# Gains moved from the weight tiles to the activations, and weight tiles split in pairs

## The chip, the core and the metric

One Trainium2 chip, one of its cores. Five engines of the core work at the same time, each through its own instructions in a fixed order: the tensor engine (PE, with its weight loads PEld), the vector engine (DVE), the scalar engine (ACT), GpSimd (POOL) and SyncE (SP), which here issues every DMA. An engine whose next instruction waits for another engine, or for a DMA, does nothing in the meantime, even when later instructions could run. Data lies in HBM, in SBUF (128 partitions) and, for the tensor engine's results, in PSUM. The metric is the time of one execution on the device in microseconds (us); less is better.

## The reference

Two layers of a decoder on 256 tokens of width 2048, all in float32. Each layer is a mixer and an FFN, each between two RMS norms with gains:

```python
h = rms_norm(x, g_mix_pre)                    # x * rsqrt(mean x^2) * gain
proj = h @ w_in                               # 2048 x 11776
u_pool, u_conv, q, k, v, g_ret, gate_pre = jnp.split(proj, IN_OFFSETS, axis=-1)
y_pool = pool_mixer(u_pool, pool_w, pool_scale) @ w_pool_proj   # ends in "* pool_scale"
y_conv = conv_module(u_conv, ...) @ w_conv_proj
y_ret = retention(q, k, v, g_ret, positions, ret_gn_g) @ w_ret_proj   # ends in "* gn_g", silu(gate)
merged = gates[:, :, 0] * y_pool + gates[:, :, 1] * y_conv + gates[:, :, 2] * y_ret
x = x + rms_norm(merged @ w_out, g_mix_post)
h = rms_norm(x, g_ffn_pre)
a, b = jnp.split(h @ w_ffn_in, 2, axis=-1)    # 2048 x 11264
x = x + rms_norm((jax.nn.silu(a) * b) @ w_ffn_out, g_ffn_post)
```

Four of these gains stand directly ahead of a product with a weight matrix: `g_mix_pre`, `g_ffn_pre`, `pool_scale` and `ret_gn_g`. Such a gain has one factor for each row of the matrix, so it can go on the activation's column or on the weight's row.

## The kernel before, in words

The weights, 2048 tiles of 128 rows x 512 columns, are read once in the order in which they are used. `fetch` (line 602) brings two row tiles at a time (512 KB, one DMA) into one of 4 buffers `raw`. `load` (line 611) splits each tile into two parts in the narrower format float32r: ACT writes the high part `whi`, DVE the rest, `wlo`. Where the rows have a gain, ACT multiplies by it while it writes `whi` (line 623) and DVE does so while it subtracts (line 624); the other tiles take lines 620 and 621. 13 buffers of each part are kept.

The activations stand transposed, also split: `split` (line 122) makes a high part on ACT (line 124) and a rest on DVE (line 125) of four blocks of 128 x 128, a *quad*, which `transpose4` (line 128) has put into PSUM with four products by the identity. A float32 product is then three products, `multiply` (line 637): activation high with `whi` (line 648), high with `wlo` (line 649), low with `whi` (line 650). Each takes 128 tokens; the two halves of the tokens are called h = 0 and h = 1, and h = 1 follows 7 to 8 tiles behind h = 0 (`LAG`), so that what lies between two sub-layers for one half is done beside products of the other.

Between two sub-layers, `post_norm` (line 177) adds up squares, lets POOL make the factor `rpost` (lines 117 and 119), and DVE updates `x` in four blocks of 512 columns (line 185); each block is then transposed and split to a quad of the new `xT`. The conv, pooling and retention work is cut into small jobs that are put between the products.

The order on each engine is made by a scheduler from the program and its own estimates, except for the first 16 tiles (`begin`, line 661), where the program's order is kept for PE, ACT, DVE and SP; but instructions of later parts can still be placed among them. One of these is the conversion of the token positions, `posf` (line 210), for the rotary tables. Its input `posi` comes by two small DMAs (line 208). At the start, SP issues DMAs for `x`, the first weights, parameters (`par`), pooling tables (`dt`) and gains (`gp`). Eight are in flight at the most: from the ninth on, each DMA's issue waits until the one eight places before it has landed.

Of the kernel before, what the change touches and what calls it, by code (L numbers as in the profile page):

```python
# [37 lines left out]
WBUFS = 13  # L38
# [32 lines left out]
def trunk(ctx: ExitStack, tc: tile.TileContext, x, positions, g_mix_post, g_ffn_post, w_in, pool_w,  # L71
# [50 lines left out]
    def split(src):  # L122
        t = slot([P, 2, 4, P], F32R)
        act.copy(t[:, 0], src)  # L124
        dve.tensor_tensor(t[:, 1], src, t[:, 0].bitcast(F32), op=ALU.subtract)  # L125
        return t
# [25 lines left out]
    def pre_norm_quad(h, c):  # L152
        st["xT", h].append(split(transpose4(xs[h][:, c, :])))
# [15 lines left out]
    def post_collect(h, c, src, bc):  # L169
        """One 512 column block of a sub-layer's output: kept times its gain, squares summed."""  # L170
# [6 lines left out]
    def post_norm(h, final):  # L177
# [5 lines left out]
        def residual(c):  # L183
            xc = xs[h][:, c, :]
            dve.scalar_tensor_tensor(xc, ogs[c], r, xc, op0=ALU.mult, op1=ALU.add)  # L185
            if final:
                nc.sync.dma_start(out[0, h * P:(h + 1) * P, c * NB:(c + 1) * NB], xc)

        if final:
            for c in range(4):  # L190
                residual(c)
            return
        st["xT", h] = []
        residual(0)
        for c in range(4):
            defer(N_FIRST + N_STEP * c, pre_norm_quad, h, c)
# [131 lines left out]
    def pool_job(l, h):  # L328
# [21 lines left out]
        st["brT", 0, h] = [split(ps)]  # L350
        yield 1.4

    def ret_job(l, h, qd):
# [50 lines left out]
        st["brT", 2, h][qd] = split(transpose4(m))  # L404
# [111 lines left out]
    def ev_out(l, c):  # L516
        def f(h, ps):
# [3 lines left out]
            if c == 3:  # L521
                post_norm(h, False)
# [19 lines left out]
    def ev_ffn(l, c, part, last):  # L542
        def f(h, ps):
# [9 lines left out]
            if c == 3:  # L553
                post_norm(h, l + 1 == DEPTH)
        return f

# [4 lines left out]
    def add(w, r0, kt, c0, lhs, evac, gain=None, needs=()):  # L561
        chunks.append((w, r0, kt, c0, lhs, evac, gain, needs))

    for l in range(DEPTH):
        wi = w_in[l]
        gpre, gffn = par[l][:, C_GPRE:C_GPRE + 16], par[l][:, C_GFFN:C_GFFN + 16]
        add(wi, 0, 16, Q_POOL, "xT", ev_pool(l), gpre)
        for qd in range(2):
            add(wi, 0, 16, Q_V + qd * NB, "xT", ev_v(qd), gpre)
        for qd in range(2):  # L570
            add(wi, 0, 16, Q_Q + qd * NB, "xT", ev_rot("qT", qd), gpre)
        for qd in range(2):
# [29 lines left out]
    def fetch(i):  # L602
# [5 lines left out]
        for kk in range(LOAD):  # L608
            raws[i + kk] = raw[:, kk, :]
# [150 lines left out]
```

## Time and profile before

| | |
|---|---|
| median of 3 runs | 2905.14 us (2904.59 to 2905.62) |
| span of the profiled execution (the only time it has) | 2904.9 us |
| PE busy | 2882.4 us, 99% of the span |
| DVE busy | 1896.8 us, 65% |
| ACT busy | 1631.0 us, 56% |
| DMA | 190 GB/s in the mean |
| mean granted clock of the tensor engine | 0.999 |

A group's row gives line, engine, operation, tiles as "written<-read", shapes and count, then the busy time and the mean of one, then the idle time of that engine just before them and what ended most of it. The timeline gives start and duration of single instructions; two that follow each other on one engine overlap by some 0.1 us, so what an instruction costs its engine is the distance between two starts. The busy time of PE says little about what could be saved: its products overlap.

### The profile page before, as it was taken

Reading aid. Unit: us, or ns where it says so; the run is one execution under the profiler, and the core shown is the slowest. Engines: PE = TensorE matmul, PEld = TensorE weight load, DVE = VectorE, ACT = ScalarE, POOL = GpSimd, SP = SyncE. Lnnn points to the kernel's source line nnn. Section 1 sums busy time; section 2 is a strip of 40 time slices with the busy share of each in tenths; the row PEclk is TensorE's granted clock in tenths of the full one; section 3 lists DMA queues with packets and bytes.
Section 4 is the critical chain, followed back from the end, with each engine's and each line's share of the span. In section 5 each row is a group of like instructions: output and inputs, shape, how many; then the busy total and the mean of one; then the engine's idle time right before and its main releaser. Section 6 shows DMA issues by size and latency. Waiting matters only on the chain.

```text
span 2904.9 us, 36969 instructions
## 1 busy us (share of the span) xinstructions
PE 2882.4 (99%) x13072; PEld 2389.0 (82%) x13072; DVE 1896.8 (65%) x2925; ACT 1631.0 (56%) x2477; POOL 87.8 (3%) x94
## 2 busy tenths in 40 slices
PE   8999999999999999999999999999999999999998
PEld 7888888888888888888888888888888888888887
DVE  6667976666666555666566679766666665556655
ACT  6555556555655545555565555565565555455553
POOL 0000000110000000000000000001000000000000
PEclk9999999999999999999999999999999999999999
DMA  7666666656666656665666656666556665566654
GB/s 245 193 187 179 185 203 188 189 188 202 182 189 189 189 195 193 189 191 190 203 186 187 186 173 188 201 184 195 190 184 197 189 190 189 195 190 190 189 197 148
DMA packets 287689, 553.14 MB, mean 190 GB/s; under 512 B 17680, under 2 KB 18960, under 8 KB 287504
## 3 DMA queue, kind: packets, MB, share of 16 engines
q1 hardware_dynamic: 287504, 550.79, 62.7%
q8 instruction: 102, 1.67, 0.2%
q14 instruction: 83, 0.68, 0.1%
HBM read 548.62 MB, written 2.10 MB: 190 GB/s over the span
## 4 chain that ended last, share of the span: by engine, by line
PE 97%; DVE 1%; DMA 0%; POOL 0%; issue 0%; ACT 0%; SPq 0%; DVEq 0%; POOLq 0%; ACTq 0%
PE mm L650 32%; PE mm L648 32%; PE mm L649 32%; PE tp L131 2%; DVE wlo L624 0%; DVE x L185 0%; PE sc L387 0%; PE tp L379 0%; DMA x<-in_x 0%; PE sc L343 0%; DVE slot L175 0%; DMA dt<-in_bands 0%; POOL rpost_a L117 0%; POOL rpost L119 0%; PE sc L349 0%
## 5 line engine op out<-in xcount | busy, mean ns | idle before, releaser
L648 PE MATMUL mm<-whi,slot 128*128 128x512 f32 x4096 | 1606.9, 392 | 0.0
L650 PE MATMUL mm<-whi,slot 128*128 128x512 f32 x4096 | 1597.3, 390 | 0.0
L649 PE MATMUL mm<-wlo,slot 128*128 128x512 f32 x4096 | 1596.3, 390 | 0.0
L623 ACT ACTIVATE whi<-raw,par 128x512 fp32r<-128x512 f32 x1536 | 1110.0, 725 | 822.2 <-PE mm L650 787.4
L624 DVE SCALAR_TENSOR_TENSOR wlo<-raw,par,whi 128x512 fp32r<-128x512 f32 x1536 | 1162.0, 761 | 603.9 <-ACT whi L623 585.9
L650 PEld LDWEIGHTS mm<-whi,slot 128*128 128x128 f32 x4096 | 769.3, 188 | 161.0 <-DVE slot L125 0.6
L649 PEld LDWEIGHTS mm<-wlo,slot 128*128 128x128 f32 x4096 | 769.9, 188 | 156.1 <-DVE wlo L624 0.4
L648 PEld LDWEIGHTS mm<-whi,slot 128*128 128x128 f32 x4096 | 769.9, 188 | 155.8 <-ACT slot L124 0.7
L621 DVE TENSOR_TENSOR wlo<-raw,whi 128x512 fp32r<-128x512 f32 x512 | 355.3, 695 | 294.3 <-ACT whi L620 293.1
L620 ACT CAST whi<-raw 128x512 fp32r<-128x512 f32 x512 | 319.0, 623 | 332.8 <-DVE wlo L621 240.1
L301 DVE SCALAR_TENSOR_TENSOR slot<-slot,par,slot 128x252 f32<-128x252 f32 (+19 forms) x240 | 104.6, 466 | 0.4
L125 DVE TENSOR_TENSOR slot<-tp,slot 128x512 fp32r<-128x512 f32 x100 | 68.3, 687 | 24.0 <-ACT slot L124 23.9
L124 ACT CAST slot<-tp 128x512 fp32r<-128x512 f32 x100 | 57.5, 578 | 31.9 <-PE tp L131 31.8
L496 POOL TENSOR_TENSOR slot<-slot,tb 128x512 f32<-128x512 f32 x32 | 55.8, 1745 | 633.6 <-DVE tb L495 615.4
L117 POOL TENSOR_SCALAR rpost_a<-ssq_t 128x1 f32<-128x1 f32 x8 | 4.1, 513 | 1610.2 <-DVE ssq_t L179 1610.2
L483 ACT ACTIVATE sg<-mm,rstd 128x512 f32<-128x512 f32 x48 | 33.1, 690 | 15.0 <-PE mm L650 14.9
L529 DVE SCALAR_TENSOR_TENSOR sg<-mm,rstd,tb 128x512 f32<-128x512 f32 x44 | 32.9, 748 | 12.7 <-ACT tb L527 12.7
L131 PEld LDWEIGHTS tp<-ident,ta 128*128 128x128 f32 x272 | 34.0, 142 | 8.4
L131 PE MATMUL tp<-ident,ta 128*128 128x128 f32 x272 | 40.6, 271 | 0.0
L537 DVE SCALAR_TENSOR_TENSOR ta<-mm,rstd,sg 128x512 f32<-128x512 f32 x44 | 32.9, 747 | 9.6 <-PE mm L650 9.5
L527 ACT ACTIVATE tb<-mm,rstd 128x512 f32<-128x512 f32 x44 | 30.4, 690 | 14.1 <-PE mm L650 14.1
L131 PE MATMUL tp<-ident,x 128*128 128x128 f32 x128 | 20.6, 289 | 10.8 <-DMA x<-in_x 7.3
(104 smaller groups left out, 469.9 us busy)
## 6 DMA issues: line engine op xcount, KB each, us to landing
raw<-in_w_in SPq DMA_DIRECT2D x368, 512.0 KB, 3.7
raw<-in_w_ffn_in SPq DMA_DIRECT2D x352, 512.0 KB, 3.8
raw<-in_w_ffn_out SPq DMA_DIRECT2D x176, 512.0 KB, 3.6
raw<-in_w_out SPq DMA_DIRECT2D x64, 512.0 KB, 3.7
raw<-in_w_ret_proj SPq DMA_DIRECT2D x32, 512.0 KB, 4.1
raw<-in_w_pool_proj SPq DMA_DIRECT2D x16, 512.0 KB, 3.8
raw<-in_w_conv_proj SPq DMA_DIRECT2D x16, 512.0 KB, 4.2
dt<-in_decays SPq DMA_DIRECT2D x12, 256.0 KB, 4.0
```

What stands on the lines that cost most here:

```text
L124: act.copy(t[:, 0], src)
L125: dve.tensor_tensor(t[:, 1], src, t[:, 0].bitcast(F32), op=ALU.subtract)
L131: pe.transpose(tp[:, j, :], src[:, j * P:(j + 1) * P], ident)
L301: dve.scalar_tensor_tensor(acc[:, ct, s:], hT[:, ct, :SEQ - s], w[:, TAPS - 1 - s:TAPS - s], acc[:, ct, s:], op0=ALU.mult, op1=ALU.add)
L496: gp.tensor_tensor(m, m, t, op=ALU.add)
L620: act.copy(hi, raw)
L621: dve.tensor_tensor(lo, raw, hi.bitcast(F32), op=ALU.subtract)
L623: act.activation(hi, raw, ACT.Identity, scale=gain[:, k:k + 1])
L624: dve.scalar_tensor_tensor(lo, raw, gain[:, k:k + 1], hi.bitcast(F32), op0=ALU.mult, op1=ALU.subtract)
L648: pe.matmul(ps, ah, hi, start=(k == 0), stop=False)
L649: pe.matmul(ps, ah, lo, start=False, stop=False)
L650: pe.matmul(ps, al, hi, start=False, stop=(k == kt - 1))
```

## The change

Line numbers below are those of the changed kernel where they stand with rows of it.

1. **Gains go on the activations.** `split` takes a `gain`; where it has one, DVE first writes `u = src * gain` (128 x 512, one instruction, the gain repeated along the columns) into SBUF (line 127), and ACT (line 129) and DVE (line 130) then split `u`. This is so for the 32 quads of `xT` (8 at each of 4 sub-layers), for the 4 of the pooling branch and the 8 of the retention branch.
2. **Weight tiles are split in pairs.** `load` takes the whole of `raw`: one ACT copy (line 621) and one DVE subtraction (line 622) of 128 x 1024. There are 1024 of each in place of 2048.
3. **Buffers.** 7 blocks of two tiles of `whi` and of `wlo`, 14 tiles in place of 13. A block comes free when h = 1 has used both of its tiles.

```diff
-    def split(src):
+    def split(src, gain=None):
         t = slot([P, 2, 4, P], F32R)
+        if gain is not None:
+            u = t2("ta", 3, (P, 4, P))
+            dve.tensor_tensor(u, src, gain.unsqueeze(2).to_broadcast([P, 4, P]), op=ALU.mult)
+            src = u
         act.copy(t[:, 0], src)
         dve.tensor_tensor(t[:, 1], src, t[:, 0].bitcast(F32), op=ALU.subtract)
         return t
...
-    def load(i):
-        n, k = items[i]
-        gain = chunks[n][6]
+    def load():
+
+        i = loaded[0]
         if i not in raws:
             fetch(i)
         raw = raws.pop(i)
-        hi = wpool.tile([P, NB], F32R, name=nm("whi"), tag="whi", bufs=WBUFS)
-        lo = wpool.tile([P, NB], F32R, name=nm("wlo"), tag="wlo", bufs=WBUFS)
-        if gain is None:
-            act.copy(hi, raw)
-            dve.tensor_tensor(lo, raw, hi.bitcast(F32), op=ALU.subtract)
-        else:
-            act.activation(hi, raw, ACT.Identity, scale=gain[:, k:k + 1])
-            dve.scalar_tensor_tensor(lo, raw, gain[:, k:k + 1], hi.bitcast(F32), op0=ALU.mult, op1=ALU.subtract)
-        wt[i] = (hi, lo)
-
-    ahead = [WBUFS]
+        hi = wpool.tile([P, LOAD, NB], F32R, name=nm("whi"), tag="whi", bufs=WBLOCKS)
+        lo = wpool.tile([P, LOAD, NB], F32R, name=nm("wlo"), tag="wlo", bufs=WBLOCKS)
+        act.copy(hi, raw)
+        dve.tensor_tensor(lo, raw, hi.bitcast(F32), op=ALU.subtract)
+        for kk in range(LOAD):
+            wt[i + kk] = (hi[:, kk, :], lo[:, kk, :])
+        loaded[0] += LOAD
+
+    ahead = [LOAD * WBLOCKS]
...
     def load_ahead():
-        load_next(max(0, min(len(items), done[1] + ahead[0]) - loaded[0]))
+        while loaded[0] < min(len(items), done[1] // LOAD * LOAD + ahead[0]):
+            load()
```

The scheduler's order changes with it at a few places. **First, SP at the start**, from its thirteenth DMA on. Before (`raw_N` is a pair of weight tiles, `x_80` and `x_81` are h = 0 and h = 1 of `x`):

```order
L205 DMA par_83<-in_params 128x180
L607 DMA raw_182<-in_w_in 128x2x512
L167 DMA x_81<-in_x 128x512
L607 DMA raw_210<-in_w_in 128x2x512
L167 DMA x_80<-in_x 128x512
L607 DMA raw_244<-in_w_in 128x2x512
L167 DMA x_81<-in_x 128x512
L607 DMA raw_272<-in_w_in 128x2x512
L208 DMA posi<-in_positions 128x1 x2
```

and now:

```order
L210 DMA par_83<-in_params 128x180
L213 DMA posi<-in_positions 128x1 x2
L610 DMA raw_178<-in_w_in 128x2x512
L172 DMA x_81<-in_x 128x512
L511 DMA gp_5160<-in_g_mix_post 128x512
L610 DMA raw_204<-in_w_in 128x2x512
L172 DMA x_80<-in_x 128x512
```

The two DMAs of `posi` moved from behind the last weights of the start to the places right behind `par_83`, and the gains `gp` moved forward too.

**Second, DVE at the start.** Before, from its second computing instruction on (`tp` is a transposed quad in PSUM, `slot` a split one; `posf` comes as the twentieth row):

```order
L125 TENSOR_TENSOR slot_98<-tp_93,slot_98 128x512
L624 SCALAR_TENSOR_TENSOR wlo_102<-raw_88,par_82,whi_101 128x512
L624 SCALAR_TENSOR_TENSOR wlo_106<-raw_88,par_82,whi_105 128x512
L125 TENSOR_TENSOR slot_114<-tp_109,slot_114 128x512
L624 SCALAR_TENSOR_TENSOR wlo_122<-raw_91,par_82,whi_121 128x512
L624 SCALAR_TENSOR_TENSOR wlo_126<-raw_91,par_82,whi_125 128x512
L125 TENSOR_TENSOR slot_145<-tp_140,slot_145 128x512
```

and now:

```order
L127 TENSOR_TENSOR ta_99<-tp_93,par_82 128x512
L130 TENSOR_TENSOR slot_98<-ta_99,slot_98 128x512
L622 TENSOR_TENSOR wlo_104<-raw_88,whi_103 128x1024
L127 TENSOR_TENSOR ta_113<-tp_107,par_82 128x512
L130 TENSOR_TENSOR slot_112<-ta_113,slot_112 128x512
L215 CAST posf<-posi 128x2
L622 TENSOR_TENSOR wlo_122<-raw_91,whi_121 128x1024
L127 TENSOR_TENSOR ta_142<-tp_136,par_82 128x512
L130 TENSOR_TENSOR slot_141<-ta_142,slot_141 128x512
L622 TENSOR_TENSOR wlo_149<-raw_118,whi_148 128x1024
```

Each quad has a second DVE instruction, and `posf` moved from the twentieth row to the seventh, ahead of the second pair's `wlo`.

**Third, DVE between the first mixer and the first FFN**, from the last gain product of h = 0 on. Before (`x_80` is updated by columns of 512, `tp_6644` is the first transposed quad):

```order
L175 TENSOR_TENSOR slot_6414<-mm_6425,gp_6600 128x512
L179 TENSOR_REDUCE ssq_t_6605<-ssq_o_6039 128x1
L624 SCALAR_TENSOR_TENSOR wlo_6616<-raw_6591,par_82,whi_6615 128x512
L185 SCALAR_TENSOR_TENSOR x_80<-slot_6038,rpost_6609,x_80 128x512
L624 SCALAR_TENSOR_TENSOR wlo_6625<-raw_6622,par_82,whi_6624 128x512
L624 SCALAR_TENSOR_TENSOR wlo_6632<-raw_6622,par_82,whi_6631 128x512
L624 SCALAR_TENSOR_TENSOR wlo_6641<-raw_6638,par_82,whi_6640 128x512
L125 TENSOR_TENSOR slot_6649<-tp_6644,slot_6649 128x512
L185 SCALAR_TENSOR_TENSOR x_80<-slot_6038,rpost_6609,x_80 128x512
```

and now:

```order
L180 TENSOR_TENSOR slot_5474<-mm_5481,gp_5628 128x512
L184 TENSOR_REDUCE ssq_t_5633<-ssq_o_5163 128x1
L622 TENSOR_TENSOR wlo_5649<-raw_5646,whi_5648 128x1024
L190 SCALAR_TENSOR_TENSOR x_80<-slot_5162,rpost_5637,x_80 128x512
L622 TENSOR_TENSOR wlo_5661<-raw_5658,whi_5660 128x1024
L127 TENSOR_TENSOR ta_5670<-tp_5664,par_82 128x512
L190 SCALAR_TENSOR_TENSOR x_80<-slot_5162,rpost_5637,x_80 128x512
L622 TENSOR_TENSOR wlo_5684<-raw_5681,whi_5683 128x1024
L130 TENSOR_TENSOR slot_5669<-ta_5670,slot_5669 128x512
L127 TENSOR_TENSOR ta_5693<-tp_5687,par_82 128x512
L190 SCALAR_TENSOR_TENSOR x_80<-slot_5474,rpost_5637,x_80 128x512
```

A block of `wlo` and the new product `ta` now stand between two updates of `x_80`, and another block ahead of the quad's low part. On PE the first transposes of `x_80` there moved 7 products back, to 4 products ahead of the end of h = 1's sub-layer, and the second ones moved 2 products forward, ahead of the first product of the new sub-layer instead of behind its second. At the other two transitions both come to stand at the same places. Over the whole program PE keeps its products; their order differs at these places and, by single products, in the first 60 us.

More of the change, by code (lines that the diff above doesn't have):

```diff
@@ L37 @@
 LAG = 7
-WBUFS = 13
+WBLOCKS = 7
 SLOTS = 22
@@ L150, in tick, with pre_norm_quad @@
             fn(*args)
-    def pre_norm_quad(h, c):
-        st["xT", h].append(split(transpose4(xs[h][:, c, :])))
+    def pre_norm_quad(h, c, gain):
+        st["xT", h].append(split(transpose4(xs[h][:, c, :]), gain[:, 4 * c:4 * c + 4]))
     def pre_norm_rstd(h, ssq):
@@ L175, in post_collect, with post_norm @@
         dve.tensor_tensor(o, src, bc, op=ALU.mult)
-    def post_norm(h, final):
+    def post_norm(h, gain):
         tot = small("ssq_t", 1)
@@ L185, in residual @@
             dve.scalar_tensor_tensor(xc, ogs[c], r, xc, op0=ALU.mult, op1=ALU.add)
-            if final:
+            if gain is None:
                 nc.sync.dma_start(out[0, h * P:(h + 1) * P, c * NB:(c + 1) * NB], xc)
-        if final:
+        if gain is None:
             for c in range(4):
@@ L195, in post_norm @@
         for c in range(4):
-            defer(N_FIRST + N_STEP * c, pre_norm_quad, h, c)
+            defer(N_FIRST + N_STEP * c, pre_norm_quad, h, c, gain)
             if c < 3:
@@ L349, in pool_job @@
             pe.matmul(ps[:, g, :], pw[:, g, :], pT[:, g, :], start=True, stop=True)
-        st["brT", 0, h] = [split(ps)]
+        st["brT", 0, h] = [split(ps, par[l][:, C_PS:C_PS + 4])]
         yield 1.4
@@ L403, in ret_job @@
         yield WAIT
-        st["brT", 2, h][qd] = split(transpose4(m))
+        st["brT", 2, h][qd] = split(transpose4(m), par[l][:, C_GN + 4 * qd:C_GN + 4 * qd + 4])
         yield 1.2
@@ L521, in f @@
             if c == 3:
-                post_norm(h, False)
+                post_norm(h, par[l][:, C_GFFN:C_GFFN + 16])
         return f
@@ L553, in f @@
             if c == 3:
-                post_norm(h, l + 1 == DEPTH)
+                post_norm(h, par[l + 1][:, C_GPRE:C_GPRE + 16] if l + 1 < DEPTH else None)
         return f
@@ L588, in trunk @@
             for j in range(b0, b1):
-                add(w_ffn_in[l], 0, 16, j * NB, "xT", ev_a, gffn)
-                add(w_ffn_in[l], 0, 16, HIDDEN + j * NB, "xT", ev_b(j == b0), gffn)
+                add(w_ffn_in[l], 0, 16, j * NB, "xT", ev_a)
+                add(w_ffn_in[l], 0, 16, HIDDEN + j * NB, "xT", ev_b(j == b0))
             for c in range(4):
@@ L607, in fetch @@
         nc.sync.dma_start(raw, w[r:r + LOAD * P, c0:c0 + NB].rearrange("(k p) n -> p k n", p=P))
-        for kk in range(LOAD):
-            raws[i + kk] = raw[:, kk, :]
-    def load(i):
-        n, k = items[i]
-        gain = chunks[n][6]
+        raws[i] = raw
+    def load():
+        i = loaded[0]
         if i not in raws:
@@ L639, in multiply @@
         n, k = items[i]
-        w, r0, kt, c0, lhs, evac, gain, needs = chunks[n]
+        w, r0, kt, c0, lhs, evac, needs = chunks[n]
         if k == 0:
@@ L661, in begin @@
     def begin():
+        gain = par[0][:, C_GPRE:C_GPRE + 16]
         load_x(0, 0)
@@ L666, in begin @@
         fetch(2)
-        pre_norm_quad(0, 0)
-        load_next(2)
+        pre_norm_quad(0, 0, gain)
+        load()
         for c in range(4):
             if c == 0:
-                pre_norm_quad(1, 0)
+                pre_norm_quad(1, 0, gain)
             if c < 3:
@@ L675, in begin @@
                 load_x(1, c + 1)
-            load_next(2)
+            load()
             multiply(0)
@@ L680, in begin @@
             if c < 3:
-                pre_norm_quad(0, c + 1)
+                pre_norm_quad(0, c + 1, gain)
                 fetch(4 * c + 6)
-                load_next(2)
+                load()
             multiply(1)
             if c < 3:
-                pre_norm_quad(1, c + 1)
+                pre_norm_quad(1, c + 1, gain)
             for h in (0, 0, 1, 1):
@@ L695, in trunk @@
         begin()
-    ahead[0] = WBUFS
+    ahead[0] = LOAD * WBLOCKS
     defer(16, add_job, ("trig", 0), rotary_tables(), True)
```

30 lines of the change are left out of this document (12 added, 18 removed).

## The prediction

> **What bounds the kernel now.** I read the page's groups first, then the waits of PE, then the start and the first transition in the timeline.
>
> ```profile
> span 2904.9 us, 36969 instructions
> PE mm L650 32%; PE mm L648 32%; PE mm L649 32%; PE tp L131 2%; DVE wlo L624 0%; DVE x L185 0%; PE sc L387 0%; PE tp L379 0%; DMA x<-in_x 0%; PE sc L343 0%; DVE slot L175 0%; DMA dt<-in_bands 0%; POOL rpost_a L117 0%; POOL rpost L119 0%; PE sc L349 0%
> L648 PE MATMUL mm<-whi,slot 128*128 128x512 f32 x4096 | 1606.9, 392 | 0.0
> L623 ACT ACTIVATE whi<-raw,par 128x512 fp32r<-128x512 f32 x1536 | 1110.0, 725 | 822.2 <-PE mm L650 787.4
> L624 DVE SCALAR_TENSOR_TENSOR wlo<-raw,par,whi 128x512 fp32r<-128x512 f32 x1536 | 1162.0, 761 | 603.9 <-ACT whi L623 585.9
> L621 DVE TENSOR_TENSOR wlo<-raw,whi 128x512 fp32r<-128x512 f32 x512 | 355.3, 695 | 294.3 <-ACT whi L620 293.1
> L620 ACT CAST whi<-raw 128x512 fp32r<-128x512 f32 x512 | 319.0, 623 | 332.8 <-DVE wlo L621 240.1
> ...
> 1509.23 0.39 PE L648 MATMUL mm<-whi,slot 128*128 128x512 f32 x1
> 1510.59 0.39 PE L648 MATMUL mm<-whi,slot 128*128 128x512 f32 x1
> ...
> PE tp L131 <- DMA x<-in_x: 7.3, 2, 3.7
> PE tp L131 <- DVE x L185: 3.6, 6, 0.9
> PE sc L343 <- DMA dt<-in_bands: 1.7, 1, 1.7
> ```
>
> The chain that ends last is PE's three products, 96%. Six products lie between the two L648 rows, so one costs 1.36 / 6 = 0.227 us, and 3 x 4096 of them 2786 us of 2904.9. The split that the change makes cheaper is not on that chain: ACT idles 787 us in front of L623 because PE still holds the buffers, DVE idles behind ACT. PE's waits are 12.6 us in all. 7.3 is the first arrival of `x`, which stays. The 3.6 us are six waits at the three transitions (two each, 1.2 us). So the change cannot gain more than about 3.6 us, whatever it saves on DVE and ACT; it can lose where it makes PE wait anew. The span agrees with the median of the runs (2905.14) to 0.01%. A measurement of this kernel tells about 0.2% (5.8 us) from no change.
>
> **What is removed, and hidden.** 1536 + 512 splits on each engine become 1024 of 128 x 1024. No row has that shape; I extend rows:
>
> ```profile
> L457 DVE TENSOR_TENSOR tb<-mm,tr 128x256 f32<-128x256 f32 x16 | 6.6, 415 | 0.0
> L456 DVE TENSOR_TENSOR ta<-mm,tr 128x512 f32<-128x512 f32 x16 | 11.1, 691 | 6.9 <-PE mm L650 6.9
> L136 ACT ACTIVATE junk<-x 128x512 f32<-128x512 f32 x32 | 20.3, 633 | 6.4 <-DVE x L185 6.1
> L248 ACT ACTIVATE sin<-slot 128x128 f32<-128x128 f32 x1 | 0.3, 312 | 0.0
> L124 ACT CAST slot<-ta 128x512 fp32r<-128x512 f32 x4 | 2.6, 646 | 0.0
> ```
>
> DVE takes (691 - 415) / 256 = 1.08 ns a column, so 1024 columns take 695 + 512 x 1.04 to 1.08 = 1.23 us (bounds: 1.06 if the fixed part vanished, 1.39 if it doubled). ACT takes (633 - 312) / 384 = 0.84 ns a column: 623 + 428 = 1.05 us (bounds 0.99, 1.25). DVE's sum falls by 1536 x 0.761 + 512 x 0.695 - 1024 x 1.23 = 265 us, ACT's by about 354. Worth to the end: nothing, since PE's products hide it. Their cover is wide: a pair's buffers come free 4 tiles of both halves ahead of their next use, 24 products or 5.4 us, against 1.05 + 1.23 and one instruction in front on each engine, about 3.7. The 14 tiles in place of 13 let the first tile of a pair start when it did.
>
> **What is added: 44 products by the gain on DVE.** They read PSUM with a repeated factor, as L456 does: 0.69 us, 30 us in all. ACT then reads SBUF (646 ns). The 12 of pooling and retention lie beside PE's products; if they were late, each costs 0.7 us. The 32 of `xT` stand on a path that PE waits for.
>
> **The start: a wait that was harmless comes to the front.**
>
> ```profile
> 6.70 1.33 ACT L623 ACTIVATE whi<-raw,par 128x512 fp32r<-128x512 f32 x2 [1.31 <-DMA raw<-in_w_in]
> 9.61 0.33 SPq L205 DMA_DIRECT2D par<-in_params  x1
> 11.05 0.38 SPq L607 DMA_DIRECT2D raw<-in_w_in  x1
> 12.35 0.33 SPq L167 DMA_DIRECT2D x<-in_x  x1
> 19.22 0.94 SPq L208 DMA_DIRECT2D posi<-in_positions  x2
> ...
> DMA to landing us min/median/max: 2.6/4.9/7.1
> ...
> DMA to landing us min/median/max: 4.6/4.8/4.9
> ...
> 14.20 0.59 ACT L124 CAST slot<-tp 128x512 fp32r<-128x512 f32 x1 [2.88 <-PE tp L131]
> 15.07 0.48 PE L648 MATMUL mm<-whi,slot 128*128 128x512 f32 x1
> 15.38 0.39 PE L649 MATMUL mm<-wlo,slot 128*128 128x512 f32 x1
> 25.08 0.16 DVE L210 CAST posf<-posi 128x2 f32<-128x2 int32 x1
> 27.80 0.47 PE L648 MATMUL mm<-whi,slot 128*128 128x512 f32 x1
> ```
>
> The landing rows are of `par` (2.6 for the first, 7.1 for the one issued at 9.61, since the first was in use at 6.70) and of `posi`. Before, `posi` was issued at 19.2 and read at 25.08 without a wait. Now its two DMAs take the next two places behind `par`, where SP issued at 11.05 and 12.35, behind all the data of the start. `par` lands at 9.61 + 7.1 = 16.7; `posi`, behind it, between 12.35 + 4.6 = 16.95 and 12.35 + 7.1 = 19.45. I take 17.0, because `par`'s landing shows when that backlog is through. `posf` now stands on DVE ahead of the second pair's `wlo`, so DVE is blocked until then. Behind it wait that `wlo` (17.2 to 18.4), the next quad's gain product, ACT's cast of that quad and the following pair, and SP's next weights, whose buffer that pair holds. PE wants this `wlo` at 15.38 and gets it at 18.4: 3.0 us.
>
> From there the start becomes a chain. In it the engines take turns: gain product 0.69, cast (the next ACT instruction starts some 0.56 later), `whi` 1.05, `wlo` with 1.13 until the next DVE instruction, and three hand-overs of 0.03: 3.5 us a pair. Six pairs (the third to the eighth) end at 18.35 + 6 x 3.5 = 39.4. Before, PE asked for the eighth pair's `wlo` at 27.80 + 25 x 0.227 = 33.5. The start thus costs **5.9 us** (3.3 us a pair and 16.95: 4.7; 3.7 us and 19.45: 9.5). Without `posf` the chain would begin with the transposes at 14.2 and end at 35.2: 1.7 us. Behind the start, four pairs share ACT with the squares of `x`, and the pooling's first products stand one product earlier, so that its table DMA is covered less: 0.3 + 0.2 us.
>
> **The transitions: DVE has more to do exactly there.**
>
> ```profile
> 715.05 0.15 DVE L179 TENSOR_REDUCE ssq_t<-ssq_o 128x1 f32<-128x4 f32 x1
> 715.12 0.74 DVE L624 SCALAR_TENSOR_TENSOR wlo<-raw,par,whi 128x512 fp32r<-128x512 f32 x1
> 716.58 0.75 DVE L185 SCALAR_TENSOR_TENSOR x<-slot,rpost,x 128x512 f32<-128x512 f32 x1 [0.71 <-POOL rpost L119]
> 717.47 0.63 PE L131 MATMUL tp<-ident,x 128*128 128x128 f32 x4 [0.90 <-DVE x L185]
> 719.23 0.68 DVE L125 TENSOR_TENSOR slot<-tp,slot 128x512 fp32r<-128x512 f32 x1
> 719.83 0.74 DVE L185 SCALAR_TENSOR_TENSOR x<-slot,rpost,x 128x512 f32<-128x512 f32 x1
> 728.10 1.06 PE L131 MATMUL tp<-ident,x 128*128 128x128 f32 x8 [0.26 <-DVE x L185]
> ```
>
> Between the last product of h = 0 and the steady state DVE had 11 `wlo` at 0.66 from start to start; it has 6 blocks at 1.13 and 8 gain products at 0.60: 7.3 us become 11.6. In the new order PE meets four waits in place of its 0.90 + 0.26. (1) The first block of `x` is ready at about 718.2, a block of `wlo` standing in front of it; PE, now 7 products later, is there at 718.0: 0.2. (2) Between the first and the second update of `x` stand a block and a gain product, 0.66 + 1.13 + 0.60 = 2.39 us from start to start; PE has 4 products and 4 transposes, 1.4 us: 1.0. (3) The low part of the first quad stands behind another block, 1.13, and the update, 0.66, and PE wants it two products after its high part: 0.7. (4) The third quad has its gain product behind a block and the first update of h = 1: 0.9. Together 2.8 against 1.2: **+1.6** at each of three, 4.8 us. Bounds: -1.2 each if the lighter splits take all waits away; +3.2 each if every wait is double.
>
> POOL's first step for `rpost` shows a price that may add to (1):
>
> ```profile
> L117 POOL TENSOR_SCALAR rpost_a<-ssq_t x8: 190/620/622, 715.3 to 2897.8; 128x1 f32<-128x1 f32 x8
> ```
>
> 190 ns alone, 620 while a `wlo` of 512 columns runs. The Trainium skill (SBUF — State Buffer, on the port pair that DVE and GpSimd share) says that a DVE instruction with two inputs in SBUF holds out a GpSimd one that reads SBUF for its whole length; the row agrees, and by that rule a block of 1.13 us would cost up to 0.5 us more at each transition, 1.5 us on the sum.
>
> **The sum.** 2904.9 + 5.9 + 0.5 + 4.8 = 2916.1; I say **2916 us**, +0.4%. The tail behind the last product has no splits and stays.
>
> **Rivals.** A: `posi` lands in time, or the wait lies in PE's slack. For it: four-byte rows are little data, and PE wants the `wlo` only at 15.38. Against: `par`, 90 KB, needed 7.1 us from a place ahead. Then 2904.9 + 1.7 + 0.5 + 4.8 = 2912; with the transitions at half their price 2909.5. Chance 0.18.
>
> B, on the other side: the freed engines decide. DVE and ACT lose 235 and 350 us of work, pairs are split sooner, and the transitions lose their waits: 2904.9 - 3.6, and with an early `posi` whose chain runs at 3.2 us a pair (14.2 + 19.2 = 33.4, no wait) 2901 to 2905. It decides once a transition's `x` updates come less than 1.4 us apart. Against: 7.3 us of DVE work became 11.6. Chance 0.12.
>
> C: the tensor engine's clock falls during the new gap and has to come back:
>
> ```profile
> 11.40 0.63 PE L650 MATMUL mm<-whi,slot 128*128 128x512 f32 x1
> 11.82 0.63 PE L648 MATMUL mm<-whi,slot 128*128 128x512 f32 x1
> ```
>
> At the start products cost 0.42 to 0.43 instead of 0.227, nine of them. Eight to nine such products again are 1.7 us: 2918. For it: behind the first product no gap was longer than 1.7 us so far, and this one is 3.0. TensorE: Matmul & The Clock Gate (Part 1, the Trainium skill) lets the clock halve after an idle window of about 3.4 us; a gap of 3.0 would just escape, one of 4 would not. Chance 0.15.
>
> The forecast itself has 0.55; with costs of 5 to 16 us its own range is 2910 to 2920. The range of all reaches down into A and up past C: **2907 to 2921**. Slower by over 0.2% (above 2910.7): 0.85 of the forecast, C, and 0.45 of A, about 0.69. Faster (below 2899.3) asks for more than all of PE's waits at the transitions: 0.03. Same: 0.28.
>
> **What would show it.** Right, if DVE idles about 5 us ahead of `posf`, ended by the DMA of `posi`, PE waits about 3 us for the `wlo` that follows, products still come 0.227 apart, DVE's busy sum is near 1660 and ACT's near 1280 us, and PE's waits on `x`, on `ta` and its low part at 720 to 730 us are near 8 us for the three transitions. Wrong, if `posf` doesn't wait, if the second update of `x` is there before PE, or if products at 400 to 700 us wait for `whi` or `wlo`, which I take to be covered.

## The result, and the profile after

| | before | after |
|---|---|---|
| median on the device | 2905.11 us (2904.59 to 2905.62, 4 runs) | 2917.26 us (2916.77 to 2917.70, 4 runs) |
| span of the profiled execution | 2904.9 us | 2914.7 us |
| DVE busy | 1896.8 us | 1702.8 us |
| ACT busy | 1631.0 us | 1286.0 us |
| PE busy | 2882.4 us | 2885.5 us |

The change made the kernel slower by 12.15 us: ratio 1.0042, 95% interval 1.0028 to 1.0056. The forecast was 2916 us, 1.3 us too low.

The page of the changed kernel: span, busy times, the chain that ended last, and the groups of the splits and of the products.

```profile
span 2914.7 us, 34024 instructions
PE 2885.5 (99%) x13072; PEld 2388.8 (82%) x13072; DVE 1702.8 (58%) x1945; ACT 1286.0 (44%) x1453; POOL 90.8 (3%) x94
PE 96%; DVE 2%; ACT 1%; DMA 1%; POOL 0%; issue 0%; SPq 0%; DVEq 0%; POOLq 0%; ACTq 0%
L622 DVE TENSOR_TENSOR wlo<-raw,whi 128x1024 fp32r<-128x1024 f32 x1024 | 1270.8, 1242 | 998.7 <-ACT whi L621 997.9
L621 ACT CAST whi<-raw 128x1024 fp32r<-128x1024 f32 x1024 | 1078.6, 1053 | 1362.5 <-PE mm L646 1335.4
```

DVE and ACT lost 194 and 345 us of work, and none of it came off the end: ACT's idle time in front of `whi` that PE ends, which holds the buffers, grew from 877 us (787 in front of line 623, 90 in front of line 620) to 1335 us. About half of the 12 us is in PE's listed waits, 19.0 us in place of 12.6 (us in total, times, longest):

```profile
PE tp L136 <- DMA x<-in_x: 6.8, 2, 3.6
PE tp L136 <- DVE x L190: 4.8, 7, 0.8
PE mm L645 <- DVE wlo L622: 4.6, 2, 4.1
PE mm L644 <- DVE x L190: 1.3, 2, 0.6
PE mm L646 <- DVE slot L130: 0.8, 2, 0.4
PE sc L348 <- DMA dt<-in_bands: 0.5, 1, 0.5
PE mm L644 <- ACT slot L129: 0.2, 1, 0.2
```

New are 4.6 us for `wlo` (4.1 at the start, 0.5 at 48.8 us), and 3.5 us more for `x` and what is made of it (4.8 + 1.3 + 0.8 + 0.2 in place of 3.6). The wait for the table `dt` fell from 1.7 to 0.5 us. The start in the timeline of the changed kernel (start, duration, engine and line):

```profile
10.28 1.70 SPq L213 DMA_DIRECT2D posi<-in_positions  x2
...
10.46 0.69 DVE L130 TENSOR_TENSOR slot<-ta,slot 128x512 fp32r<-128x512 f32 x1 [0.68 <-ACT slot L129]
16.44 0.17 DVE L215 CAST posf<-posi 128x2 f32<-128x2 int32 x1 [5.29 <-DMA posi<-in_positions]
16.55 1.22 DVE L622 TENSOR_TENSOR wlo<-raw,whi 128x1024 fp32r<-128x1024 f32 x1
20.00 1.22 DVE L622 TENSOR_TENSOR wlo<-raw,whi 128x1024 fp32r<-128x1024 f32 x1 [0.26 <-ACT whi L621]
...
13.29 0.48 PE L644 MATMUL mm<-whi,slot 128*128 128x512 f32 x1
17.83 0.79 PE L645 MATMUL mm<-wlo,slot 128*128 128x512 f32 x1 [4.05 <-DVE wlo L622]
18.42 0.63 PE L646 MATMUL mm<-whi,slot 128*128 128x512 f32 x1
...
20.55 0.59 PE L645 MATMUL mm<-wlo,slot 128*128 128x512 f32 x1
20.98 0.39 PE L646 MATMUL mm<-whi,slot 128*128 128x512 f32 x1
```

DVE stands still for 5.29 us with nothing but two numbers per partition to convert; the block that PE waits for comes right behind. Behind the gap PE's products are 0.43 us apart until 20.98, and the next `wlo` starts 3.45 us after the one before.

The first transition of the changed kernel, DVE, then PE and POOL:

```profile
720.86 1.22 DVE L622 TENSOR_TENSOR wlo<-raw,whi 128x1024 fp32r<-128x1024 f32 x1 [0.15 <-ACT whi L621]
722.53 0.75 DVE L190 SCALAR_TENSOR_TENSOR x<-slot,rpost,x 128x512 f32<-128x512 f32 x1 [0.44 <-POOL rpost L120]
723.20 1.22 DVE L622 TENSOR_TENSOR wlo<-raw,whi 128x1024 fp32r<-128x1024 f32 x1
724.33 0.68 DVE L127 TENSOR_TENSOR ta<-tp,par 128x512 f32<-128x512 f32 x1
724.93 0.74 DVE L190 SCALAR_TENSOR_TENSOR x<-slot,rpost,x 128x512 f32<-128x512 f32 x1
...
722.52 0.39 PE L645 MATMUL mm<-wlo,slot 128*128 128x512 f32 x1
723.43 0.63 PE L136 MATMUL tp<-ident,x 128*128 128x128 f32 x4 [0.52 <-DVE x L190]
725.82 0.63 PE L136 MATMUL tp<-ident,x 128*128 128x128 f32 x4 [0.84 <-DVE x L190]
727.47 0.50 PE L646 MATMUL mm<-whi,slot 128*128 128x512 f32 x1 [0.41 <-DVE slot L130]
733.85 0.51 PE L644 MATMUL mm<-whi,slot 128*128 128x512 f32 x1 [0.62 <-DVE x L190]
...
721.07 1.42 POOL L120 TENSOR_TENSOR rpost<-rpost_a,nhalf 128x1 f32<-128x1 f32 x1
```

Between two updates of `x` (722.53 and 724.93) lie a block and a gain product, 2.40 us. PE waits four times, 2.4 us in the view. What a wait costs is more than the view lists: from 722.52 to 723.43 are 0.91 us where 0.227 is the pace, so the 0.52 cost 0.68: the view lists a product with 0.39 us, 0.16 more than the pace, and counts a wait from the listed end.

### The profile page after: what moved, and what is told of

The parts are those of the page before. It is cut to its first block, busy times and chain, and to the rows that moved or that the text cites. A ratio compares the mean times of both kernels' runs of the same rounds, so it can differ in the third digit from the quotient of the medians.

```text
span 2914.7 us, 34024 instructions
## 1 busy us (share of the span) xinstructions
PE 2885.5 (99%) x13072; PEld 2388.8 (82%) x13072; DVE 1702.8 (58%) x1945; ACT 1286.0 (44%) x1453; POOL 90.8 (3%) x94
## 3 DMA queue, kind: packets, MB, share of 16 engines
q8 instruction: 102, 1.67, 0.2%
## 4 chain that ended last, share of the span: by engine, by line
PE 96%; DVE 2%; ACT 1%; DMA 1%; POOL 0%; issue 0%; SPq 0%; DVEq 0%; POOLq 0%; ACTq 0%
PE mm L646 31%; PE mm L645 31%; PE mm L644 31%; PE tp L136 2%; DVE wlo L622 1%; DVE x L190 0%; ACT whi L621 0%; DVE ta L127 0%; DMA raw<-in_w_in 0%; PE sc L392 0%; PE tp L384 0%; POOL rpost L120 0%; PE sc L348 0%; DVE slot L180 0%; DMA posi<-in_positions 0%
## 5 line engine op out<-in xcount | busy, mean ns | idle before, releaser
L622 DVE TENSOR_TENSOR wlo<-raw,whi 128x1024 fp32r<-128x1024 f32 x1024 | 1270.8, 1242 | 998.7 <-ACT whi L621 997.9
L621 ACT CAST whi<-raw 128x1024 fp32r<-128x1024 f32 x1024 | 1078.6, 1053 | 1362.5 <-PE mm L646 1335.4
L306 DVE SCALAR_TENSOR_TENSOR slot<-slot,par,slot 128x251 f32<-128x251 f32 (+17 forms) x240 | 102.9, 482 | 0.5
L129 ACT CAST slot<-tp 128x512 fp32r<-128x512 f32 x60 | 35.2, 587 | 54.2 <-PE tp L136 53.6
L130 DVE TENSOR_TENSOR slot<-tp,slot 128x512 fp32r<-128x512 f32 x60 | 41.4, 691 | 20.4 <-ACT slot L129 17.3
L129 ACT CAST slot<-ta 128x512 fp32r<-128x512 f32 x48 | 29.5, 621 | 47.6 <-DVE ta L127 46.4
L130 DVE TENSOR_TENSOR slot<-ta,slot 128x512 fp32r<-128x512 f32 x48 | 32.7, 687 | 8.9 <-ACT slot L129 8.9
L500 DVE TENSOR_TENSOR tb<-mm,sg 128x512 f32<-128x512 f32 x32 | 22.1, 690 | 19.1 <-PE mm L646 18.8
```

Source lines behind the costliest of these rows:

```text
L306: dve.scalar_tensor_tensor(acc[:, ct, s:], hT[:, ct, :SEQ - s], w[:, TAPS - 1 - s:TAPS - s], acc[:, ct, s:], op0=ALU.mult, op1=ALU.add)
L621: act.copy(hi, raw)
L622: dve.tensor_tensor(lo, raw, hi.bitcast(F32), op=ALU.subtract)
```

## The experiments

Theory: two things cost the time, the early cast on DVE (about 4 us) and the separate gain product, which lengthens the engines' turns at the start and DVE's queue at the transitions (about 6.5 us); splitting in pairs costs nothing. Rivals: the pairs cost by their length; the clock costs; the cast lies in slack. All times below are medians, and "+" is against the runs of the kernel before made beside them (2904.83, 2904.96 and 2905.14 us in the three groups; 27 or 28 runs each). The changed kernel stands at +12.15. The intervals reach 2.5 to 3.3 us to either side, so a difference of 1 or 2 us between two kernels rests on their traces as much as on their times.

**1. The cast on POOL** (`posf_pool`).

```diff
-        dve.tensor_copy(posf, posi)
+        gp.tensor_copy(posf, posi)
```

> The change, with the cast of the positions (posf) on POOL in place of DVE; the two position DMAs keep their place in SP's queue. Theory: the cast's 5.3 us wait on the DMA is what moved the second pair's low part and, through the queue behind it, the start; without it PE gets that low part at about 15.5 us, the clock no longer falls, and of the start only the longer turn of the engines (about 1.7 us) is left, while the transitions keep their waits (2.3 to 2.4 us on PE each). 2917.3 - 4.2 - 1.4 = about 2911.5, between 2910.5 and 2913.5. Rival 1, the wait lay in slack (the second pair would be late anyway, because the gain products and the pairs take turns on ACT and DVE): 2916 to 2917.5. Rival 2, only the clock matters: the wait on the low part stays, the slow products go, 2915.5 to 2916.

Measured: 2913.13 us, +8.30 (ratio 1.0028, 1.0017 to 1.0038): 3.85 us of 12.15 are gone. The time is in the theory's range, 1.6 us above its middle, and the first rival falls. The products behind 13.4 us come at full pace, so the wait and the fall of the clock went together; the second rival, by which the wait stays and only the slow products go, falls too. What remains of the start is mostly in gaps that the waits do not list. The timeline of this kernel, DVE and PE:

```profile
26.09 1.23 DVE L622 TENSOR_TENSOR wlo<-raw,whi 128x1024 fp32r<-128x1024 f32 x1 [0.26 <-ACT whi L621]
27.23 0.68 DVE L127 TENSOR_TENSOR ta<-tp,par 128x512 f32<-128x512 f32 x1
28.60 0.69 DVE L130 TENSOR_TENSOR slot<-ta,slot 128x512 fp32r<-128x512 f32 x1 [0.69 <-ACT slot L129]
29.56 1.23 DVE L622 TENSOR_TENSOR wlo<-raw,whi 128x1024 fp32r<-128x1024 f32 x1 [0.26 <-ACT whi L621]
...
32.43 0.40 PE L645 MATMUL mm<-wlo,slot 128*128 128x512 f32 x1
32.82 0.50 PE L646 MATMUL mm<-whi,slot 128*128 128x512 f32 x1
33.16 0.40 PE L644 MATMUL mm<-whi,slot 128*128 128x512 f32 x1
33.39 0.39 PE L645 MATMUL mm<-wlo,slot 128*128 128x512 f32 x1
```

A pair takes 3.47 us, as in the chain of the forecast, and PE runs right behind it: products 0.39 and 0.34 us apart where 0.23 is the pace. The view by windows counts what PE started from 16 to 46 us (the number behind its busy time, transposes included). In the kernel before, then in this one:

```profile
16.00:46.00 30.00, 30.00 (x141) 24.46 (x140) 20.77 (x36) 23.61 (x48) 1.49 (x4) 1.00 0.80 252
```

```profile
16.00:46.00 30.00, 29.40 (x130) 21.78 (x128) 20.94 (x24) 19.77 (x34) 2.71 (x3) 1.00 0.77 245
```

The 11 that are missing are about 2.5 us at 0.227 each. The view of waits has one of 0.5 us there.

**2. The kernel before with the cast early** (`before_early_posf`).

```diff
+                if c == 0:
+                    fetch(6)
+                    load_x(0, 2)
+                    nc.sync.dma_start(par[1], params[1])
+                    posi = cpool.tile([P, 2], I32, name="posi")
+                    for h in range(2):
+                        nc.sync.dma_start(posi[:, h:h + 1], positions[0, h * P:(h + 1) * P].unsqueeze(1))
+                    st["posf"] = cpool.tile([P, 2], F32, name="posf")
+                    dve.tensor_copy(st["posf"], posi)
                 load_next(2)
```

> The kernel before, in which only the positions come early: the second row of parameters and the two position DMAs stand on SP behind the first ten DMAs of the start (as in the changed kernel), and the cast posf stands on DVE ahead of the second pair's low parts. Splits, gains and buffers are those of before. Theory: the wait costs by itself, whatever the splits are. posi lands at about 16.5 to 17.0 us, the low part 0.9 us later, PE wants it at 13.5 to 15.4: 2.5 to 4.0 us, and 1.4 us of slow products if the gap makes the clock fall; behind it no chain, since a pair's turn on DVE is 1.9 us here. 2904.8 + 2.5 to 5.4 = 2907.3 to 2910.2. Rival: it costs only where the gain product and the 1024 column block stand behind it, and is hidden here: 2904 to 2906.

Measured: 2906.94 us, +1.98 (ratio 1.0007, 0.9998 to 1.0016): just under the theory's range and outside the rival's. The start of this kernel in the timeline:

```profile
8.02 1.72 SPq L678 DMA_DIRECT2D posi<-in_positions  x2
...
15.15 0.17 DVE L680 CAST posf<-posi 128x2 f32<-128x2 int32 x1 [4.64 <-DMA posi<-in_positions]
...
16.03 0.50 PE L644 MATMUL mm<-wlo,slot 128*128 128x512 f32 x1 [1.29 <-DVE wlo L619]
16.36 0.40 PE L645 MATMUL mm<-whi,slot 128*128 128x512 f32 x1
16.60 0.40 PE L643 MATMUL mm<-whi,slot 128*128 128x512 f32 x1
```

SP issued the two DMAs 2.3 us earlier than in the changed kernel, so the cast ended 1.3 us earlier, and one `wlo` of 512 columns (0.66 us) stood in front of PE in place of 1.13. PE waited 1.29 us, and the clock did not fall. So the wait is there without pairs and without gain products. That it also costs time by itself rests on the trace, since the interval holds 1; how much it costs depends on where PE is when DVE comes free.

**3. The gain products left out** (`no_gain_posf_pool`, then `no_gain_dt3_posf_pool`).

```diff
-        if gain is not None:
+        if False:
...
-            b = t2("dt", 2, (P, 4, P))
+            b = t2("dt", 3, (P, 4, P))
```

The second piece of the diff is in the second kernel alone, at each use of `dt`; that kernel also has two buffers for `ta` in place of three. Both kernels leave the gains out altogether, so they tell about time and do not compute the reference.

> As posf_pool, and the product by the gain is left out of the split of the activations, so the four gains (pre-norm, feed-forward, pooling, retention) are in no factor at all; the weights are still split in pairs of 1024 columns in 7 blocks. Theory: the 32 gain products on the way from x to PE carry the transitions (0.60 us each on DVE) and the longer turns at the start; without them PE waits at a transition as before (about 1.2 us, between 0.5 and 1.5) and the start costs nothing: 2904 to 2907. Rival, the pairs themselves do it (an update of x stands behind 1.13 us of a block in place of 0.66): PE's waits at a transition stay above 1.8 us, 2908 to 2911.

Measured: 2908.00 us, +3.17 (ratio 1.0010, 1.0001 to 1.0019): at the lower edge of the rival's range, above the theory's. The waits decided against both: at the three transitions PE waited less than before, and the 3 us were a table that came late. Waits and timeline of this kernel:

```profile
PE sc L348 <- DMA dt<-in_bands: 3.3, 1, 3.3
PE tp L136 <- DVE x L190: 2.1, 4, 0.8
...
53.20 2.34 PE L348 MATMUL sc<-dt,slot 128*128 128x128 f32 x14 [3.33 <-DMA dt<-in_bands]
...
56.20 0.63 PE L644 MATMUL mm<-whi,slot 128*128 128x512 f32 x1
56.62 0.63 PE L645 MATMUL mm<-wlo,slot 128*128 128x512 f32 x1
```

So it was run again with a third buffer for that table:

> As no_gain_posf_pool (the gains are in no factor at all), with three buffers for the pooling tables dt in place of two and two for ta in place of three. In no_gain_posf_pool PE waited 3.3 us for the third table near 53 us, seven products behind it took 0.43 us, and at the three transitions PE lost 0.3 us less each than in the kernel before. Theory: pairs of 1024 columns by themselves cost nothing, and gain a little at the transitions; with the third table in time, 2908.0 - 3.3 - 1.4 = 2903.3, between 2902 and 2905. Rival (pairs and 7 blocks cost 2 to 3 us somewhere else): 2906 to 2908.

Measured: 2902.53 us, -2.61 (ratio 0.9991, 0.9983 to 1.0000), within the theory's range. Pairs without gain products cost nothing; against the kernel before with the third buffer (experiment 6, -0.67) they are 1.9 us ahead, which is less than the intervals can tell. So what costs time in the change is the cast and the gain products, but experiment 4 shows that a part of the gain products' price is due to the pairs.

**4. Pairs or single tiles** (`tiles_posf_pool`).

```diff
-        act.copy(hi, raw)
-        dve.tensor_tensor(lo, raw, hi.bitcast(F32), op=ALU.subtract)
+        for kk in range(LOAD):
+            act.copy(hi[:, kk, :], raw[:, kk, :])
+            dve.tensor_tensor(lo[:, kk, :], raw[:, kk, :], hi[:, kk, :].bitcast(F32), op=ALU.subtract)
```

> As posf_pool, with the splits done one tile of 512 columns at a time (two casts and two subtractions per block, the same seven blocks, gains on the activations). Tells pairs from gain products. Theory (the sum of DVE's work between a transition's last product and its steady state decides): singles take 2 x 0.66 = 1.32 us where a pair takes 1.13, so the transitions are no cheaper, PE waits 2.0 to 3.2 us at each, and the time is that of posf_pool or up to 2 us more. Rival (the length of the one instruction in front of an update or a gain product decides): PE waits about 1.2 us at each, and the time is 3 us below posf_pool.

Measured: 2912.18 us, +7.35 (ratio 1.0025, 1.0015 to 1.0035), 0.95 below `posf_pool`: between the two, and nearer the theory. The waits at the transitions were 2.5, 3.6 and 2.5 us, as the theory had it (2.0 to 3.2) and a little above; the rival's 1.2 is excluded. The trace shows two effects that neither named in full. At the three transitions PE lost 1.5 us more than in `posf_pool`, and from 16 to 46 us it lost 2.2 us less: its window there has 145 starts in place of 130. With single tiles the gain product costs next to nothing at the start, so the slow chain there needs both, the separate product and the long blocks.

**5. The product elsewhere** (`act_gain_posf_pool`, `fused_posf_pool`). The first gives the product to ACT behind the start; the second does without it.

```diff
+            if clock[0] > 64:
+                for j in range(4):
+                    act.activation(u[:, j, :], src[:, j, :], ACT.Identity, scale=gain[:, j:j + 1])
+            else:
+                dve.tensor_tensor(u, src, gain.unsqueeze(2).to_broadcast([P, 4, P]), op=ALU.mult)
```

> As posf_pool, but behind the start the gain product of the activations is done by ACT, as four scaled copies of 128 columns (about 0.31 us each, 1.25 us for four), and DVE's queue is rid of it at the transitions. Theory (DVE's queue decides): the waits for the second update of x and for the third quad fall by 0.60 us or more each; the high part of a quad comes up to 0.6 us later, which PE's products of the other half cover; PE waits 1.0 to 1.6 us at a transition, and the time is 2 to 4 us below posf_pool. Rival (the length of the way from x over the transposes to the split decides, on whatever engine it runs): PE waits as much as in posf_pool or up to 1 us more at each, and the time is the same or up to 3 us above.

Measured: 2910.58 us, +5.75 (ratio 1.0020, 1.0011 to 1.0028), 2.55 below `posf_pool`, in the theory's range. PE's waits at the transitions were 1.6, 2.3 and 1.6 us; the second one gained nothing by this view. So DVE's queue decides, but in part only: by the two traces 1.3 us were gained at the transitions, and 0.9 us between 46 and 75 us, where the theory named nothing and the wait for the table fell from 1.2 to 0.3 us.

```diff
         if gain is not None:
+            for j in range(4):
+                act.activation(t[:, 0, j, :], src[:, j, :], ACT.Identity, scale=gain[:, j:j + 1])
+            for j in range(4):
+                dve.scalar_tensor_tensor(t[:, 1, j, :], src[:, j, :], gain[:, j:j + 1], t[:, 0, j, :].bitcast(F32),
+                                         op0=ALU.mult, op1=ALU.subtract)
+            return t
```

> As posf_pool, with no separate product by the gain: ACT makes the high part of a quad as four scaled copies of 128 columns, and DVE its low part as four scalar_tensor_tensor of 128 columns, (value x gain) - high, straight from PSUM. DVE then spends about 4 x 0.29 = 1.15 us on a quad where it spent 0.60 + 0.68 = 1.28, but nothing of it stands between the transposes and the high part. Theory (what counts is DVE's work ahead of an update of x and of the high part): waits as in act_gain_posf_pool, 1.2 to 2.0 us at a transition, 2909 to 2912. Rival (the sum of DVE's work in a transition counts): as posf_pool, 2912.5 to 2914.

Measured: 2906.94 us, +1.98 (ratio 1.0009, 1.0000 to 1.0018), better than either expected. The expectation had looked at the transitions alone. There the waits fell to 1.1, 2.4 and 1.1 us, where the kernel before has 1.2, 1.3 and 1.2; and at the start the product is out of the engines' turns as well: from 16 to 46 us PE waited for nothing, by this kernel's windows with 146 starts in place of 130:

```profile
16.00:46.00 30.00, 30.00 (x146) 24.83 (x146) 21.62 (x40) 23.37 (x48) 2.67 (x5) 1.00 0.88 278
```

The lines of this kernel's first transition show the shorter way between two updates of `x`, 1.81 us for 2.40:

```profile
715.52 0.75 DVE L193 SCALAR_TENSOR_TENSOR x<-slot,rpost,x 128x512 f32<-128x512 f32 x1 [0.44 <-POOL rpost L120]
716.19 1.22 DVE L625 TENSOR_TENSOR wlo<-raw,whi 128x1024 fp32r<-128x1024 f32 x1
717.33 0.75 DVE L193 SCALAR_TENSOR_TENSOR x<-slot,rpost,x 128x512 f32<-128x512 f32 x1
```

**6. More cover, and the losses taken away** (`lag8_posf_pool`, `before_lag8_dt3`, `before_dt3`, `fused_dt3_posf_pool`).

```diff
-LAG = 7
+LAG = 8
-N_FIRST, N_STEP = 5, 2
+N_FIRST, N_STEP = 6, 2
```

> As posf_pool, with the second half of the tokens 8 tiles behind the first in place of 7, and the quads of x one tile later (N_FIRST 6 in place of 5), still 7 blocks of two tiles. Theory (the waits at the transitions are a lack of cover): PE has three products more, 0.68 us, before it asks for the first quad of each half; the chain of waits of the first half (0.5 + 0.8 + 0.4) falls to about 1.1 us, the one of the second half (0.6) to 0: 1.1 us for 2.4 at each, 2913.1 - 3.9 = 2909.2, between 2908.5 and 2911. Rival (the blocks come free one tile later for their next use, 6 tiles ahead in place of 7, and products wait for whi or wlo all along): 2913 or more, and waits for wlo outside the transitions. Second rival (PE's order shifts with it, and DVE's work stands where it stood): 2912.5 to 2913.5.

Measured: 2913.67 us, +8.71 (ratio 1.0031, 1.0019 to 1.0042). The theory falls: the waits at the transitions were 2.4, 2.6 and 2.4 us, as with a lag of 7. The program puts the updates of `x` off by the same count as the quads, so DVE's work moves along with PE's and no cover is gained. That is neither rival's reason: the second had DVE's work stand still, and the time is 0.2 us over its range; the first has the time in its range, but of its waits for `whi` or `wlo` all along only one shows, 0.7 us for `whi`.

> The kernel before with three buffers for the pooling tables dt in place of two, and the second half 8 tiles behind the first, the quads one tile later (N_FIRST 6). Asks whether the little that PE waits for in the kernel before is to be had without touching the splits: 1.7 us for dt near 51 us and 1.2 us at each of three transitions. Theory: both fall away, 2904.8 - 1.7 - 3.6 = 2899.5, between 2899 and 2902. Rival: the third table's DMA is late by SP's queue and not by its buffer, and with 13 buffers and a lag of 8 tiles the tiles come free too late: 2904 to 2910.

Measured: 2903.87 us, -1.09 (ratio 0.9996, 0.9987 to 1.0004). The wait for the table is gone; the waits for `x` fell only from 3.6 to 2.8 us. Theory and rival both miss the time, the rival by 0.1 us.

> The kernel before with three buffers for dt in place of two, nothing else. Tells apart what the lag of 8 tiles and the third buffer did in before_lag8_dt3 (2903.9). Theory: the third table is worth its wait, 1.7 us, and the lag nothing: 2903.2, between 2902.5 and 2904. Rival (the lag gave the 1.1 us and the buffer nothing): 2904.5 to 2905.5.

Measured: 2904.47 us, -0.67 (ratio 0.9997, 0.9988 to 1.0006), between the theory and its rival. The wait of 1.7 us is not in the trace any more, and between 46 and 75 us PE lost 2.1 us less than in the trace of the kernel before. Why the time fell by less is open. That trace is of an execution 1.7 us longer than the median of 82 others, so its wait may be longer than usual; no other execution of this kernel was traced.

> As fused_posf_pool, with three buffers for dt and two for ta. Asks whether the change without its three losses (the early cast on DVE, the separate gain product, the wait for the third table) is a faster kernel than the one before. PE waited 1.3 us for the table in fused_posf_pool. Theory: 2906.9 - 1.3 = 2905.6, between 2904.5 and 2906.5, level with before, since the transitions still cost 1 to 2 us each. Rival (two buffers for ta hold up the rotations): 2907 or more. Second rival (the shorter DVE instructions also shorten the waits elsewhere): below 2904.

Measured: 2905.14 us, 0.00 (ratio 1.0001, 0.9992 to 1.0009), as the theory said; two buffers for `ta` hold nothing up. Freed of the cast, the separate product and the wait for the table, the change is level with the kernel before. Against the kernel before with the same third buffer it is 0.7 us behind, within the intervals, and by the traces its transitions still lose 1.9 us more. The lowest times with the gains in place are the kernel before with a third buffer, without and with the lag of 8; their intervals hold 1, so neither is shown to be faster.

## Why the prediction was right, step by step

The differences of the runs add up: 3.85 us for the cast on DVE (`posf_pool`), 6.32 from a separate gain product to one folded into the split (`posf_pool` to `fused_posf_pool`), 1.98 for what is left, together 12.15. The sum of the forecast goes by places instead, so the traces are the fairer measure. The table has what PE lost in three stretches: the distance between the starts of its instructions, less the steady 0.227 us between two products (0.11 between two short ones). Some loss around transposes is in all kernels, so only differences between rows count.

| PE's loss, us (one execution each) | 16 to 46 us | 46 to 75 us | three transitions |
|---|---|---|---|
| before | 0.8 | 2.5 | 8.0 |
| `before_dt3` | 0.8 | 0.4 | 8.1 |
| changed | 7.5 | 2.3 | 13.0 |
| `posf_pool` | 3.3 | 1.9 | 13.0 |
| `tiles_posf_pool` | 1.0 | 1.8 | 14.6 |
| `act_gain_posf_pool` | 3.2 | 1.0 | 11.7 |
| `fused_posf_pool` | 0.5 | 2.0 | 9.9 |
| `fused_dt3_posf_pool` | 0.4 | 0.3 | 10.0 |
| `no_gain_posf_pool` | 0.4 | 5.7 | 7.1 |
| `no_gain_dt3_posf_pool` | 0.4 | 0.6 | 7.2 |

The first 16 us are left out: there the loss differs from 9.0 to 10.9 us between executions, by when the products reach full pace. With them, the changed kernel lost 4.9 us more than the kernel before up to 46 us (5.9 forecast), 0.1 less from 46 to 75 us (0.5 more forecast), and 5.0 more at the transitions (4.8 forecast).

- **Bound.** Right. PE sets the end, DVE and ACT gave back nothing, and behind the start one wait for `whi` or `wlo` is listed, 0.5 us at 48.8 us, beside the squares of `x` on ACT. The durations of the new shapes were extended to 1.23 and 1.05 us; they are 1242 and 1053 ns.
- **DVE's busy sum**, 1660 expected, is 1702.8. The rows of the splits fell by 1162.0 + 355.3 - 1270.8 = 246.5 where 265 was said: the blocks took 12 us more, and counts times means gave 7 us too much for what was there before. Nearly all of the other 24 us is overlap: the durations of all DVE instructions sum to 217.5 us less, but the fewer and longer ones overlap by 65 us in all instead of 88. None of it costs time.
- **The cast.** Right in place and size; rival A, a `posi` that lands in time, fell. DVE waited 5.29 us, the `wlo` came at 17.8 instead of 18.4. PE waited 4.05 instead of 3.0, because in this execution its first products reached full pace earlier (at 10.6 us; in `posf_pool`, with the same products up to there, at 13.1): it asked at 13.7, not at 15.38. So the clock did fall, which was rival C, and the forecast's sign that products still come 0.227 apart failed: seven products cost 1.4 us more, and the granted clock from 16 to 46 us (the last number but two) is 0.94, where `posf_pool` has 1.00:

```profile
16.00:46.00 30.00, 28.12 (x120) 21.89 (x121) 21.42 (x25) 17.03 (x28) 1.74 (x2) 0.94 0.67 209
```

On the end the 1.4 us do not come on top: while PE was slow, the chain of pairs behind it caught up. In `posf_pool`, without any fall, PE lost 2.5 us to the chain's pace; here about 1.5 us less. This is read from the two traces, and no run tests it. The time, 2917.26, is nearer to rival C's 2918 than to 2916. TensorE: Matmul & The Clock Gate (Part 1, the Trainium skill) puts the idle window at about 3.4 us. The traces agree with it: the clock fell behind listed idle stretches of 4.05 and 3.33 us (4.31 and 3.49 from the pace on), and not behind 1.29 or 1.67. Behind the first products no run has a stretch between 1.67 and 3.33.
- **The chain of turns.** Right in kind: 3.47 us a pair for 3.5. Its cost was 2.5 rather than 1.7 us in `posf_pool`, where the cast does not cover it. The theory of the experiments put it down to the gain product; `tiles_posf_pool` shows that it needs the long blocks as well, which stand in the forecast's turn with 1.05 and 1.13. It mostly hid from the view of waits, as a row of gaps of 0.1 us.
- **The transitions.** Four waits were named with 0.2, 1.0, 0.7 and 0.9 us; the first transition has 0.52, 0.84, 0.41 and 0.62. Their sum is 2.4 for 2.8, and each costs 0.16 more than listed, so the +1.6 is 4 x 0.16 + 2.4 - (2 x 0.16 + 1.2) = 1.5; with the small gaps it is 1.7. The first was sized too low: `rpost` came late. POOL's second step took 1.42 us beside a block of 1024 columns, 0.55 otherwise; from the sum of squares to the update of `x` were 1.96 us for 1.53. That is the 0.4 to 0.5 us that the forecast had set beside the sum. Five of the six halves paid it, and the other three waits, which were sized too high, made up for it. SBUF — State Buffer (SBUF: two separate sides, the Trainium skill) has DVE and GpSimd share a port pair that one of them holds for its whole instruction. The traces agree: beside tiles of 512 columns (`tiles_posf_pool`) the first step took 0.56 to 0.74 us, beside blocks of 1024 up to 1.17, alone 0.19. That the port pair is the cause was not tested by a run.
- **The baseline.** The sum was made against the span 2904.9, taken as equal to the runs' median. A run's time is in fact 1.7 to 2.1 us above its span (1.8 in the kernel before, 2.1 in the changed one), and that execution was a long one: 82 others of the same kernel had spans of 2901.9 to 2904.8 us, 2903.2 in the median. The two nearly cancelled, which was luck. Span against span, the change cost 9.8 us where the sum had 11.2; time against time, 12.15. So that the forecast came within 1.3 us is in part luck, while the two main places, the start and the transitions, are not.
- **The rest.** Table and squares were put at +0.5 us. The table's wait did not grow, it fell from 1.7 to 0.5 us, so that sign was wrong; the squares brought the wait of 0.5 us at 48.8 us. The 1.98 us left in `fused_posf_pool` are something else: its transitions lose 1.9 us more than before, 1.6 of them at the second one. Why that one, and why the third buffer gave 0.7 us in the kernel before and 1.8 here, where the traces show 2.1 and 1.7, was not settled.

Rival B (freed engines) had a true core: without gain products the pairs do shorten the transitions, to 0.5, 1.1 and 0.5 us of waiting. It lost because the change pays for the pairs with work on the path that PE waits for.

## What to carry to other kernels

Work taken off engines that idle is worth nothing, and work that is put on the way to the bounding engine costs time at each place where that engine waits: moving factors from 1536 hidden tiles to 44 activations added 30 us of DVE work, most of it where PE waits, and cost 7.5 us of PE's time at the start and the transitions (`posf_pool`). After such a change, look at what a scheduler has put in front of the first work of an engine in order: a conversion of two columns that waits for a DMA held DVE for 5.3 us and cost 3.9. Where a factor has to go on an activation, fold it into the two operations that already read it; here that cut the 7.5 us to about 1.6.

## What the runs showed of the hardware

- POOL's one-column steps took 190 ns alone and up to 1172 beside a block of 1024 columns on DVE (`rpost_a`), and 548 and up to 1422 (`rpost`). A longer block thus has a price on an engine that the change does not touch.
- PE's loss per wait behind a product is 0.16 us more than the idle time listed, and a bound that runs close behind shows as products 0.34 us apart in place of 0.227, with almost no wait listed: of 2.5 us between 16 and 46 us in `posf_pool` the waits have 0.5, and the count of starts in equal windows has all.
- The small DMAs of `posi` (0.5 KB each) took 4.7 to 5.9 us to land at the start, longer than the medians of those of 512 KB over the whole kernel before (3.6 to 4.2).
